# Second feed-forwards in pairs from their first block, weight splits first in each step, difference tiles 64 bytes off

## The chip, the cores and the metric

The kernel runs on one core of a Trainium2 chip. TensorE (PE) multiplies matrices from SBUF into PSUM; VectorE (DVE), ScalarE (ACT) and GpSimd (POOL) do elementwise work; SyncE (SP) issues most transfers, POOL some. The metric is the device time of one execution in microseconds. Before the change it is 2572.21 us, the median of 3 runs (2571.75 to 2572.4).

## The reference

Two layers of a hybrid decoder trunk on a 512 x 1024 fp32 input. Each layer is a half-step feed-forward, a mixer (attention and a state-space scan, whose branches are gated and merged) and a second half-step feed-forward; a last norm follows both layers.

```python
def reference(x, ...):
    for l in range(DEPTH):
        x = x + 0.5 * swiglu(rms_norm(x, ffn1_norm[l]), ffn1_w_up[l], ffn1_w_down[l])
        h = rms_norm(x, mix_norm[l])
        proj = h @ w_in[l]
        ...
        merged = jax.nn.sigmoid(gate_sb) * y_sb + jax.nn.sigmoid(gate_ssm) * y_ssm
        x = x + merged @ w_out[l]
        x = x + 0.5 * swiglu(rms_norm(x, ffn2_norm[l]), ffn2_w_up[l], ffn2_w_down[l])
    return rms_norm(x, final_norm)

def swiglu(h, w_up, w_down):
    gate, up = jnp.split(h @ w_up, 2, axis=-1)
    return (jax.nn.silu(gate) * up) @ w_down
```

D_MODEL is 1024 and the hidden width 2816, so a feed-forward has 22 hidden blocks of 128.

## The kernel before

**Tiles and precision.** x lies transposed in eight tiles of 128 channels x 512 tokens. Every fp32 product is made of three fp32r matmuls for each 128-block of the inner dimension (`mm3`, L331 to L333): high by high, high by low, low by high. So each weight unit and each input exists as a high and a low tile: whi and wlo, hhi and hlo. A unit of 128 x 1024 weights is 24 matmuls.

**Weight units.** `unit_order` lists all units of the program. `fetch` loads a unit (SP, into one of 3 wraw buffers), `convert` casts it to whi on ScalarE (L298) and, two ticks later, subtracts on VectorE to get wlo (L300); there are 3 buffers of each. When TensorE starts unit k, unit k+2 is converted, which has to wait until unit k-1 has freed its buffers.

**Blocks and pairs.** A hidden block of a feed-forward is either two units ("gate" and "up", 512 columns a matmul), or half of a pair. A pair computes gate and up of two blocks in seven products instead of eight half-width ones, each 24 matmuls of 256 columns: "11", "12", "s2", "s1", "s3", "s4", "22" in this order (`pair_of_blocks`). "11" and "12" and "s4" read the scaled input hhi, hlo; "s2", "s1", "s3" and "22" read the difference tiles th, tl, which `combine` makes from the x tiles (uv on ScalarE and VectorE, th by a cast on ScalarE L403, tl on VectorE L407). The weights of s1, s2, s3, s4 are sums: s1 and s3 are loaded as a base and a second matrix is added by an accumulating transfer that POOL issues (`onto`, L270); s2 and s4 are sums made on VectorE (`add`, L283), s4 in the tile of s2. `pairs_from` says from which block on a feed-forward uses pairs: block 6 in layer 0's first, block 2 in the others. `SLICES` cuts the 22 blocks into 8, 8 and 6; after each slice come eight "down" units that add to x.

**What sets the order.** The program is written in one order by hand. Side work (norm pieces, conversions, combines) are generators in the list `side`; `tick`, called once per three matmuls of `dense` (six in a pair's product), goes through the list in order and lets each due task emit its next instructions. Which of two tasks due in the same tick stands first on an engine is its place in the list; `spawn` puts a task at the end, or at the head with first=True. Each engine then works through its own queue in order.

**Norms.** The norm factor rs is not applied to the input but to the results (g, c), so products of the raw scaled input can start before it is known. `norm_end` (L530) sums the squares by two matmuls into pt (L541) that read rs and sq, the high and low part of acc. `dt_stage` (L809) makes decay sums in each mixer; its matmul L849 transposes sq (cum) into pt.

**Places.** hhi, hlo, whi, wlo and the act tiles start 96 bytes past a multiple of 256 in SBUF; th, tl and uv, in a pool on the right side (`open_t`), 224 past.

Of the kernel before, what the change touches and what calls it, by code (L numbers as in the profile page):

```python
# [12 lines left out]
ALU = mybir.AluOpType  # L13
# [4 lines left out]
P = 128  # L18
# [3 lines left out]
KB = DM // P  # L22
# [90 lines left out]

def pairs_from(layer, f):

    return 6 if (layer, f) == (0, 1) else 2


def unit_order(layer):

    def ffn(f):
        for s, (j0, j1) in enumerate(SLICES):
            for j in range(j0, j1):
                if j < pairs_from(layer, f):
                    yield (layer, f, "gate", j), KB
                    yield (layer, f, "up", j), KB
                elif j % 2 == 0:
                    for part in SEVEN:
                        yield (layer, f, "pair", j, part), KB
            for m in OUT_ORDER:  # L130
                yield (layer, f, "down", s, m), j1 - j0
# [32 lines left out]
class Builder:  # L164
# [7 lines left out]
    def __init__(self, ctx, tc, xT, wflat, par, taps, out):  # L172
        self.tc, self.nc = tc, tc.nc
        self.ctx = ctx
        self.xT, self.wflat, self.par, self.taps, self.out = xT, wflat, par, taps, out
        self.units, _ = all_units()
        self.keys = list(self.units)
        self.pos = 0
        self.raw, self.loaded = [], []
        self.count = 0  # L180
        self.side = []
        self.xd = None
        self.now, self.burst, self.free = 0, -1, {}
        self.sums, self.early, self.summed = {}, {}, 0
        for i, key in enumerate(self.keys):
            if key[2:] == ("gate", 0):
                first = i + 4
            if "pair" in key and key[-1] in ("s1", "s3"):
                self.early.setdefault(max(first, i - (5 if key[-1] == "s1" else 4)), []).append(key)
        self.logs = True  # L190

# [61 lines left out]
    def fetch(self, i):  # L253
        key = self.keys[i]
        raw = None
        if "pair" not in key or key[-1] in ("11", "12", "22"):
            raw = self.t(self.wraw, [P, KB * P], "wraw")
            self.nc.sync.dma_start(raw[:, :self.units[key][1] * P], self.stored(key))
            if key[-1] in ("11", "12"):
                self.sums[key] = raw  # L260
        self.raw.append(raw)
        for key in self.early.get(i, ()):
            raw = self.t(self.sx, [P, KB * P], key[-1], bufs=2)
            self.nc.sync.dma_start(raw, self.stored(key[:-1] + ("s1",)))
            self.spawn(self.onto(key, raw), 9)

    def onto(self, key, raw):

        src = self.stored(key[:-1] + ("22" if key[-1] == "s1" else "11",))
        self.nc.gpsimd.dma_start(raw, src, accum_op=ALU.add)  # L270
        self.sums[key] = raw
        yield 1

    def add(self, key):

# [10 lines left out]
    def convert(self, i):  # L286
# [5 lines left out]
        if key[-1] in ("s1", "s3"):  # L292
            raw = self.sums[key] if key[-1] == "s1" else self.sums.pop(key)
        elif key[-1] in ("s2", "s4"):
            raw = self.sums[key[:-1] + ("s2",)]
        hi = self.t(self.wsp, [P, KB * P], "whi", F32R)
        lo = self.t(self.wsp, [P, KB * P], "wlo", F32R)
# [1 line left out]
        yield 2  # L299
        nc.vector.tensor_tensor(lo[:, :n], raw[:, :n], hi[:, :n].bitcast(F32), op=ALU.subtract)  # L300
        self.loaded[i] = (hi, lo)

    def ahead(self, look=LOOK):

        last = len(self.keys) - 1
        while len(self.loaded) <= min(self.pos + look, last):
# [1 line left out]
            while len(self.raw) <= i:  # L308
                self.fetch(len(self.raw))
            self.loaded.append(None)  # L310
            self.spawn(self.convert(i))
        while len(self.raw) <= min(self.pos + self.AHEAD, last) and len(self.raw) - len(self.loaded) < 2:
            self.fetch(len(self.raw))
        for i in range(self.summed, min(self.pos + self.LOOK + 1, last) + 1):
            if self.keys[i][-1] in ("s2", "s4"):
                self.spawn(self.add(self.keys[i]))
            self.summed = i + 1

# [65 lines left out]
    def combine(self, k, gain):  # L384
# [11 lines left out]
        yield 1  # L396
        nc.vector.scalar_tensor_tensor(v[:, b], u[:, a], -1.0, v[:, b], op0=ALU.mult, op1=ALU.subtract)
        nc.vector.scalar_tensor_tensor(v[:, a], v[:, b], -1.0, v[:, a], op0=ALU.mult, op1=ALU.subtract)
        yield 2
        two = []  # L400
        for t in (u, v):
            two.append(self.t(self.tp, [P, SEQ], "th", F32R, bufs=KB))
            nc.scalar.copy(two[-1], t)  # L403
            yield 2
        for i, t, hi in zip((k, m), (u, v), two):
            lo = self.t(self.tp, [P, SEQ], "tl", F32R, bufs=KB)
            nc.vector.tensor_tensor(lo, t, hi.bitcast(F32), op=ALU.subtract)  # L407
# [176 lines left out]
    def pair_of_blocks(self, base, fp, two):  # L584
# [2 lines left out]

        nc, half, n = self.nc, SEQ // 2, KB // 2
        a, b = slice(0, half), slice(half, SEQ)
        lower, upper = self.h[:n], self.h[n:]  # L590
# [44 lines left out]

        up1, up2 = [], []
        g1, g2 = (self.t(fp, [P, SEQ], "g", bufs=4) for _ in range(2))
        product(chain, "11", lower, a, True)
        nc.scalar.copy(g1, chain)
        product(ps2, "12", upper, a, True)  # L640
        nc.vector.tensor_tensor(g1, g1, ps2, op=ALU.add)  # L641
        self.spawn(activate(g1, up1, a))
        assert None not in self.diff
        product(chain, "s2", diff[n:], b, False)
        nc.scalar.copy(g2, chain)
        product(ps3, "s1", diff[:n], a, True)
# [5 lines left out]
        product(ps3, "s4", upper, b, False)  # L652
# [104 lines left out]
    def ffn(self, layer, f, gain, gain_next):  # L757
        tc = self.tc
        with tc.tile_pool(name=f"act{layer}{f}", bufs=8, reuse_waits="tile") as ap, \
                tc.tile_pool(name=f"sx{layer}{f}", bufs=2, reuse_waits="tile") as self.sx, \  # L760
                tc.tile_pool(name=f"ffn{layer}{f}", bufs=3, reuse_waits="tile") as fp:
            self.gated = {}
            for s, (j0, j1) in enumerate(SLICES):
                act = []
                last = s == len(SLICES) - 1
                for j in range(j0, j1):
                    if j % 2 == 0:
# [1 line left out]
                        act += [tuple(t[:, i * SEQ:(i + 1) * SEQ] for t in two) for i in range(2)]  # L769
                    if j >= pairs_from(layer, f):  # L770
                        if j % 2 == 0:
                            self.pair_of_blocks((layer, f, "pair", j), fp, two)
# [36 lines left out]
    def dt_stage(self, layer):  # L809
# [36 lines left out]
        yield 2  # L846
        nc.scalar.activation(left, left, AF.Exp)
        pt = self.t(self.ptr, [P, SEQ], "pt")
        nc.tensor.transpose(pt[:n, :P], cum, self.ident)  # L849
# [558 lines left out]
    def close_t(self):  # L1408
        self.tpool.__exit__(None, None, None)
        self.tp = None  # L1410

    def build(self):
# [141 lines left out]
```

## Time and profile before

| | |
|---|---|
| median of 3 runs | 2572.21 us |
| profiled execution | 2571.97 us |
| its span | 2570.2 us |
| granted TensorE clock | 0.998 |
| first feed-forward of layer 0, span time | 0 to 352 us |
| mixer of layer 0, with its output stage from 897.28 | 352 to 940.80 us |
| second feed-forward of layer 0 | 940.80 to 1283.03 us |
| first feed-forward of layer 1 | 1283.03 to 1626.5 us |
| mixer of layer 1, with its output stage from 2171.55 | to 2215.07 us |
| second feed-forward of layer 1 | 2215.07 us to the end |

A profile comes from one execution. Its page gives busy time by engine, the chain of work that ended last, the costliest groups, and the waits of an engine with what ended them. A timeline row is: start in us, duration in us, engine, line, operation, output<-inputs, shape, count, and in brackets idle time before it and what ended it. Matmuls overlap, so the pace of TensorE is read from start to start, not from durations.

### The profile page before, as it was taken

What the parts mean: (1) busy time and instruction counts of PE and PEld (TensorE: products, weight loads), DVE (VectorE), ACT (ScalarE), POOL (GpSimd) and SP (SyncE); (2) the same over time, 40 slices, a digit from 0 to 9 for tenths busy, and PEclk for the clock granted to TensorE, in tenths of its full rate; (3) what the DMA queues carried; (4) which work ended last, traced back from release to release, by engine and by line L of the source; (5) the groups of instructions that cost most, each with busy time, mean ns of one, the idle gap of its engine ahead of it and who ended that gap; (6) DMA issues with size and microseconds to landing.
All of it is one profiled execution on the core that took longest, in us unless ns stands there. A gap on an engine that the chain in (4) does not pass through costs nothing.

```text
span 2570.2 us, 38025 instructions
## 1 busy us (share of the span) xinstructions
PE 2558.0 (100%) x15032; PEld 2290.0 (89%) x15032; DVE 1726.6 (67%) x2251; ACT 1279.1 (50%) x2103; POOL 518.8 (20%) x646
## 2 busy tenths in 40 slices
PE   9999999999999999999999999999999999999998
PEld 8898988888898889899998989888888888899997
DVE  8576875666564478586885858756666644876766
ACT  6343556665554255343553535566555533543444
POOL 0121201054342002121121312011533310122120
PEclk9999999999999999999999999999999999999999
DMA  6454442233333454555364544423333334456452
GB/s 190 131 157 139 132 139 88 87 123 103 105 109 105 141 161 134 164 140 163 108 181 140 156 140 130 141 79 102 117 98 104 116 113 142 153 142 167 140 162 82
DMA packets 104659, 335.76 MB, mean 131 GB/s; under 512 B 11872, under 2 KB 15392, under 8 KB 104480
## 3 DMA queue, kind: packets, MB, share of 16 engines
q1 hardware_dynamic: 92672, 292.84, 34.2%
q0 software_dynamic: 10944, 39.85, 8.7%
q8 instruction: 118, 1.93, 0.3%
q10 hardware_dynamic: 864, 0.64, 0.1%
q14 instruction: 61, 0.50, 0.1%
HBM read 320.60 MB, written 12.68 MB: 130 GB/s over the span
## 4 chain that ended last, share of the span: by engine, by line
PE 97%; DVE 2%; ACT 1%; DMA 0%; issue 0%; SPq 0%; DVEq 0%; ACTq 0%
PE mm L331 27%; PE mm L333 27%; PE mm L332 27%; PE pa L333 3%; PE pa L332 3%; PE pa L331 3%; PE pa L1186 2%; PE pa L1188 1%; PE pt L864 1%; PE pt L1171 1%; PE pt L1169 1%; PE pa L469 0%; PE pa L864 0%; PE pa L981 0%; DVE wlo L300 0%; PE pt L333 0%
## 5 line engine op out<-in xcount | busy, mean ns | idle before, releaser
L298 ACT CAST whi<-wraw 128x1024 fp32r<-128x1024 f32 (+3 forms) x440 | 435.2, 989 | 597.3 <-PE mm L333 488.2
L300 DVE TENSOR_TENSOR wlo<-wraw,whi 128x1024 fp32r<-128x1024 f32 (+3 forms) x440 | 538.1, 1223 | 204.7 <-ACT whi L298 203.6
L331 PE MATMUL mm<-hhi,whi 128*128 128x512 f32 (+1 forms) x1584 | 564.6, 356 | 0.0
L333 PE MATMUL mm<-hlo,whi 128*128 128x512 f32 (+1 forms) x1584 | 553.5, 349 | 0.4 <-DVE hlo L515 0.4
L332 PE MATMUL mm<-hhi,wlo 128*128 128x512 f32 (+1 forms) x1584 | 552.5, 349 | 0.0
L333 PEld LDWEIGHTS mm<-hlo,whi 128*128 128x128 f32 x1584 | 299.7, 189 | 40.4 <-DVE hlo L515 0.8
L332 PEld LDWEIGHTS mm<-hhi,wlo 128*128 128x128 f32 x1584 | 300.1, 189 | 35.2 <-DVE wlo L300 0.4
L331 PEld LDWEIGHTS mm<-hhi,whi 128*128 128x128 f32 x1584 | 300.1, 189 | 34.5 <-ACT hhi L513 0.4
L300 DVE TENSOR_TENSOR wlo<-s,whi 128x1024 fp32r<-128x1024 f32 x152 | 235.4, 1563 | 60.1 <-ACT whi L298 60.1
L331 PE MATMUL mm<-act,whi 128*128 128x512 f32 (+1 forms) x710 | 273.9, 386 | 0.0
L333 PE MATMUL mm<-act,whi 128*128 128x512 f32 (+1 forms) x710 | 273.9, 386 | 0.0
L332 PE MATMUL mm<-act,wlo 128*128 128x512 f32 (+1 forms) x710 | 273.9, 386 | 0.0
L331 PE MATMUL mm<-th,whi 128*128 128x256 f32 x912 | 257.1, 282 | 0.0
L333 PE MATMUL mm<-tl,whi 128*128 128x256 f32 x912 | 256.7, 281 | 0.0
L332 PE MATMUL mm<-th,wlo 128*128 128x256 f32 x912 | 256.5, 281 | 0.0
L634 POOL TENSOR_TENSOR g<-g,rs 128x512 f32<-128x512 f32 x76 | 132.9, 1748 | 552.5 <-DVE g L641 533.7
L298 ACT CAST whi<-s 128x1024 fp32r<-128x1024 f32 x152 | 159.3, 1048 | 102.2 <-PE mm L333 60.5
L660 DVE SCALAR_TENSOR_TENSOR x<-mm,x 128x512 f32<-128x512 f32 x93 | 64.1, 689 | 195.9 <-PE mm L333 195.9
L270 POOL DMA_DIRECT2D s<-in_wflat_dram x76 | 66.0, 868 | 616.1 <-DMA s<-in_wflat_dram 330.9
L331 PEld LDWEIGHTS mm<-th,whi 128*128 128x128 f32 x912 | 172.1, 189 | 0.0
L332 PEld LDWEIGHTS mm<-th,wlo 128*128 128x128 f32 x912 | 171.8, 188 | 0.0
L333 PEld LDWEIGHTS mm<-tl,whi 128*128 128x128 f32 x912 | 171.7, 188 | 0.0
(304 smaller groups left out, 5076.9 us busy)
## 6 DMA issues: line engine op xcount, KB each, us to landing
wraw<-in_wflat_dram SPq DMA_DIRECT2D x328, 512.0 KB, 3.6
s<-in_wflat_dram SPq DMA_DIRECT2D x76, 512.0 KB, 4.7
s<-in_wflat_dram POOLq DMA_DIRECT2D x76, 512.0 KB, 7.7
wraw<-in_wflat_dram SPq DMA_DIRECT2D x88, 384.0 KB, 3.0
cumb<-cum_d SPq DMA_DIRECT2D x16, 768.0 KB, 4.8
xd<-x SPq DMA_DIRECT2D x16, 256.0 KB, 3.1
wraw<-in_wflat_dram SPq DMA_DIRECT2D x16, 256.0 KB, 2.9
x<-xd SPq DMA_DIRECT2D x16, 256.0 KB, 3.7
```

What stands on the lines that cost most here:

```text
L270: self.nc.gpsimd.dma_start(raw, src, accum_op=ALU.add)
L298: nc.scalar.copy(hi[:, :n], raw[:, :n])
L300: nc.vector.tensor_tensor(lo[:, :n], raw[:, :n], hi[:, :n].bitcast(F32), op=ALU.subtract)
L331: mm(ps, a[0], b[0], start=start, stop=False, **kw)
L332: mm(ps, a[1], b[0], start=False, stop=False, **kw)
L333: mm(ps, a[0], b[1], start=False, stop=stop, **kw)
L634: eng.tensor_tensor(r, r, self.rs[:, cols].unsqueeze(1).to_broadcast([P, 2, half]), op=ALU.mult)
L660: self.nc.vector.scalar_tensor_tensor(x, pd, 0.5, x, op0=ALU.mult, op1=ALU.add)
L864: self.nc.tensor.transpose(pt[:, cs], src[:, cs], self.ident)
L1169: nc.tensor.matmul(pc[:, :P], bt[:, span(c)], ct[:, span(c)], start=True, stop=True)
L1171: nc.tensor.matmul(pu, btok[:, c, :], xws[c].rearrange("p h d -> p (h d)"), start=True, stop=True)
L1186: nc.tensor.matmul(py[:, i * HD:(i + 1) * HD], decs[c][:, i, :], xdts[c][:, i, :], start=True, stop=True)
```

## The change

It has five edits.

1. `pairs_from` gives 0 for the second feed-forward of each layer, so blocks 0 and 1 become a pair there. Pairs 0 and 2 are then computed in turns (`leading`): "11" and "12" of pair 0, "11" and "12" of pair 2, the other five of pair 0, the other five of pair 2. `pair_of_blocks` becomes a generator that stops behind "12" and ticks until all difference tiles exist. Pair 0 sums no weights on VectorE: s2 is a base load and two accumulating transfers, and s4 a third one onto the same tile, sent once s2 is split.
2. `ahead` spawns each conversion at the head of the task list, so in a tick that has several tasks due the weight split stands first.
3. The last `combine` has gaps of one tick instead of two.
4. `dt_stage` waits three ticks instead of two before its transpose.
5. The pool of the s tiles moves to the right side behind tpool, and a pool "rim" of 320 bytes ahead of tpool shifts th, tl and uv from 224 to 160 bytes past a multiple of 256.

```diff
 def pairs_from(layer, f):
-    return 6 if (layer, f) == (0, 1) else 2
+    return {(0, 1): 6, (1, 1): 2}.get((layer, f), 0)
+
+def leading(layer, f):
+    return [(layer, f, "pair", j, part) for j, parts in
+            ((0, SEVEN[:2]), (2, SEVEN[:2]), (0, SEVEN[2:]), (2, SEVEN[2:])) for part in parts]
...
         for s, (j0, j1) in enumerate(SLICES):
+            if s == 0 and not pairs_from(layer, f):
+                for key in leading(layer, f):
+                    yield key, KB
+                j0 = 4
...
-            if "pair" in key and key[-1] in ("s1", "s3"):
+            if key[2:] == ("pair", 0, "11"):
+                first = i - 4
+                for n, part in enumerate(("s2", "s1", "s3")):
+                    self.early.setdefault(first + n, []).append(key[:-1] + (part,))
+            elif "pair" in key and key[-2] and key[-1] in ("s1", "s3"):
...
     def onto(self, key, raw):
-        src = self.stored(key[:-1] + ("22" if key[-1] == "s1" else "11",))
-        self.nc.gpsimd.dma_start(raw, src, accum_op=ALU.add)
-        self.sums[key] = raw
-        yield 1
+        for part in {"s1": ("22",), "s3": ("11",), "s2": ("22", "11"), "s4": ("12",)}[key[-1]]:
+            self.nc.gpsimd.dma_start(raw, self.stored(key[:-1] + (part,)), accum_op=ALU.add)
+            if key[-1] != "s2" or part == "11":
+                self.sums[key] = raw
+            yield 9
...
         elif key[-1] in ("s2", "s4"):
+            while key[2:] == ("pair", 0, "s4") and key not in self.sums:
+                yield 1
             raw = self.sums[key[:-1] + ("s2",)]
...
         self.loaded[i] = (hi, lo)
+        if key[2:] == ("pair", 0, "s2"):
+            self.spawn(self.onto(key[:-1] + ("s4",), raw), 2)
...
-            self.spawn(self.convert(i))
+            self.spawn(self.convert(i), first=True)
...
-        yield 2
+        gap = 1 if m == KB - 1 else 2
+        yield gap
...
-        assert None not in self.diff
+        yield
+        while None in self.diff:
+            self.tick()
         product(chain, "s2", diff[n:], b, False)
...
         nc.scalar.activation(ecb, pt[:, n:2 * n], AF.Exp)
-        yield 2
+        yield 3
...
     def open_t(self):
+        self.rim = self.tc.tile_pool(name=self.name("rim"), bufs=1, side="right", reuse_waits="tile")
+        self.t(self.rim.__enter__(), [P, 80], "rim")
         self.tpool = self.tc.tile_pool(name=self.name("tpool"), bufs=2, side="right", reuse_waits="tile")
         self.tp = self.tpool.__enter__()
+        self.spool = self.tc.tile_pool(name=self.name("spool"), bufs=2, side="right", reuse_waits="tile")
+        self.sx = self.spool.__enter__()
```

**ScalarE at the first pair of layer 0's second feed-forward.** Before, pair 2 is the first. Names: s1, s2, s3 are the summed weights, g and c the results, and the COPY rows empty PSUM.

```order
L298 CAST whi_1633_9080<-s2_1624_9039 128x1024
L419 CAST act_1588_8883<-a_1632_9078 128x512
L639 COPY g_1630_9070<-mm_1627_9067 128x512
L298 CAST whi_1636_9113<-s1_1593_8889 128x1024
L298 CAST whi_1639_9145<-s3_1594_8891 128x1024
L645 COPY g_1631_9071<-mm_1627_9067 128x512
L612 ACTIVATE g_1630_9070<-g_1630_9070 128x512
L298 CAST whi_1643_9181<-s2_1624_9039 128x1024
L648 COPY c_1645_9204<-pa_1629_9069 128x512
```

Now, with pair 0 first (the cast that reads s2 for the second time is that of the s4 weights):

```order
L315 CAST whi_1637_9083<-s3_1538_8604 128x1024
L666 COPY g_1603_8908<-mm_1599_8904 128x512
L315 CAST whi_1639_9117<-s2_1523_8521 128x1024
L631 ACT_TABLE_LOAD
L631 ACTIVATE g_1602_8907<-g_1602_8907 128x512
L631 ACTIVATE g_1621_8993<-g_1621_8993 128x512
L669 COPY c_1641_9144<-pa_1601_8906 128x512
L315 CAST whi_1642_9152<-wraw_1636_9075 128x1024
```

Between the cast of s4 and the copy to c there now stand a table load and two activations; the cast itself reads what a POOL transfer has added to.

**POOL at the same place**, behind the last work of the mixer (gny); the DMA rows are accumulating transfers, the other rows scale a result by rs. Now:

```order
L1255 TENSOR_TENSOR gny_1385_7816<-ss_1335_7575,small_142 128x4
L284 DMA s2_1523_8521<-in_wflat_dram 128x1024
L284 DMA s1_1530_8561<-in_wflat_dram 128x1024
L284 DMA s2_1523_8521<-in_wflat_dram 128x1024
L284 DMA s3_1538_8604<-in_wflat_dram 128x1024
L284 DMA s1_1609_8946<-in_wflat_dram 128x1024
L284 DMA s2_1523_8521<-in_wflat_dram 128x1024
L653 TENSOR_TENSOR g_1602_8907<-g_1602_8907,rs_1633_9062 128x512
L653 TENSOR_TENSOR g_1621_8993<-g_1621_8993,rs_1633_9062 128x512
```

Before, two accumulates (s1 and s3 of pair 2) stood between gny and the first scaling; now there are six, the last of them for s4 of pair 0.

**VectorE at the end of layer 0's second feed-forward**, on the last residual block (x). Before:

```order
L660 SCALAR_TENSOR_TENSOR x_8501<-mm_12226,x_8501 128x512
L407 TENSOR_TENSOR tl_12299<-uv_12219,th_12256 128x512
L407 TENSOR_TENSOR tl_12307<-uv_12220,th_12265 128x512
L515 SCALAR_TENSOR_TENSOR hlo_12302<-x_8501,par_107,hhi_12301 128x512
L300 TENSOR_TENSOR wlo_12294<-wraw_12186,whi_12293 128x1024
```

And now:

```order
L681 SCALAR_TENSOR_TENSOR x_8506<-mm_12334,x_8506 128x512
L427 TENSOR_TENSOR tl_12403<-uv_12327,th_12364 128x512
L317 TENSOR_TENSOR wlo_12397<-wraw_12294,whi_12396 128x1024
L427 TENSOR_TENSOR tl_12412<-uv_12328,th_12373 128x512
L535 SCALAR_TENSOR_TENSOR hlo_12406<-x_8506,par_114,hhi_12405 128x512
```

The split (wlo) moved from behind hlo to ahead of the second tl.

**TensorE at the transpose of `dt_stage`** in layer 0 (pt<-ident,sq); the pa rows are attention scores, the mm rows the next weight unit. Before:

```order
L332 MATMUL pa_4500<-yt_4087,yt_4145 128x128
L333 MATMUL pa_4500<-yt_4088,yt_4144 128x128
L849 MATMUL pt_4509<-ident,sq_4394 96x128
L331 MATMUL mm_4512<-hhi_3573,whi_4384 128x512
L332 MATMUL mm_4512<-hhi_3573,wlo_4385 128x512
```

And now:

```order
L351 MATMUL pa_4505<-yt_4095,yt_4153 128x128
L352 MATMUL pa_4505<-yt_4096,yt_4152 128x128
L350 MATMUL mm_4514<-hhi_3578,whi_4382 128x512
L351 MATMUL mm_4514<-hhi_3578,wlo_4383 128x512
L352 MATMUL mm_4514<-hlo_3579,whi_4382 128x512
L875 MATMUL pt_4529<-ident,sq_4399 96x128
L350 MATMUL mm_4514<-hhi_3589,whi_4382 128x512
```

The transpose stands behind the first three matmuls of the unit instead of ahead of them.

More of the change, by code (lines that the diff above doesn't have):

```diff
@@ L130, in ffn @@
             for m in OUT_ORDER:
-                yield (layer, f, "down", s, m), j1 - j0
+                yield (layer, f, "down", s, m), j1 - SLICES[s][0]
     yield from ffn(1)
@@ L262, in fetch @@
         for key in self.early.get(i, ()):
-            raw = self.t(self.sx, [P, KB * P], key[-1], bufs=2)
+            raw = self.t(self.sx, [P, KB * P], key[-1], bufs=1 if key[-1] == "s2" else 2)
             self.nc.sync.dma_start(raw, self.stored(key[:-1] + ("s1",)))
@@ L314, in ahead @@
         for i in range(self.summed, min(self.pos + self.LOOK + 1, last) + 1):
-            if self.keys[i][-1] in ("s2", "s4"):
+            if self.keys[i][-1] in ("s2", "s4") and self.keys[i][-2]:
                 self.spawn(self.add(self.keys[i]))
@@ L403, in combine @@
             nc.scalar.copy(two[-1], t)
-            yield 2
+            yield gap
         for i, t, hi in zip((k, m), (u, v), two):
@@ L589, in pair_of_blocks @@
         a, b = slice(0, half), slice(half, SEQ)
-        lower, upper = self.h[:n], self.h[n:]
         diff = self.diff
@@ L637, in pair_of_blocks @@
         g1, g2 = (self.t(fp, [P, SEQ], "g", bufs=4) for _ in range(2))
-        product(chain, "11", lower, a, True)
+        product(chain, "11", self.h[:n], a, True)
         nc.scalar.copy(g1, chain)
-        product(ps2, "12", upper, a, True)
+        product(ps2, "12", self.h[n:], a, True)
         nc.vector.tensor_tensor(g1, g1, ps2, op=ALU.add)
         self.spawn(activate(g1, up1, a))
-        assert None not in self.diff
+        yield
+        while None in self.diff:
+            self.tick()
         product(chain, "s2", diff[n:], b, False)
@@ L651, in pair_of_blocks @@
         self.spawn(normed_up(c))
-        product(ps3, "s4", upper, b, False)
+        product(ps3, "s4", self.h[n:], b, False)
         nc.vector.tensor_tensor(g2, g2, ps3, op=ALU.add)
@@ L759, in ffn @@
         with tc.tile_pool(name=f"act{layer}{f}", bufs=8, reuse_waits="tile") as ap, \
-                tc.tile_pool(name=f"sx{layer}{f}", bufs=2, reuse_waits="tile") as self.sx, \
                 tc.tile_pool(name=f"ffn{layer}{f}", bufs=3, reuse_waits="tile") as fp:
@@ L763, in ffn @@
             for s, (j0, j1) in enumerate(SLICES):
-                act = []
+                act, quads = [], []
                 last = s == len(SLICES) - 1
@@ L771, in ffn @@
                         if j % 2 == 0:
-                            self.pair_of_blocks((layer, f, "pair", j), fp, two)
+                            quads.append(self.pair_of_blocks((layer, f, "pair", j), fp, two))
+                            next(quads[-1])
+                        if j % 2 == 0 and (j or pairs_from(layer, f)):
+                            for quad in quads:
+                                for _ in quad:
+                                    pass
+                            quads = []
                         continue
@@ L845, in dt_stage @@
         nc.scalar.activation(ecb, pt[:, n:2 * n], AF.Exp)
-        yield 2
+        yield 3
         nc.scalar.activation(left, left, AF.Exp)
@@ L1403, in open_t @@
     def open_t(self):
+        self.rim = self.tc.tile_pool(name=self.name("rim"), bufs=1, side="right", reuse_waits="tile")
+        self.t(self.rim.__enter__(), [P, 80], "rim")
         self.tpool = self.tc.tile_pool(name=self.name("tpool"), bufs=2, side="right", reuse_waits="tile")
         self.tp = self.tpool.__enter__()
+        self.spool = self.tc.tile_pool(name=self.name("spool"), bufs=2, side="right", reuse_waits="tile")
+        self.sx = self.spool.__enter__()
     def close_t(self):
+        self.spool.__exit__(None, None, None)
         self.tpool.__exit__(None, None, None)
+        self.rim.__exit__(None, None, None)
         self.tp = None
```

## The prediction

> **What bounds the kernel now.** I read the page's busy table first, then its chain of work that ended last, then the waits of TensorE.
>
> ```profile
> PE 2558.0 (100%) x15032; PEld 2290.0 (89%) x15032; DVE 1726.6 (67%) x2251; ACT 1279.1 (50%) x2103; POOL 518.8 (20%) x646
> PE 97%; DVE 2%; ACT 1%; DMA 0%; issue 0%; SPq 0%; DVEq 0%; ACTq 0%
> PE pt L1432 <- DVE ones L485: 1.1, 1, 1.1
> PE pt L849 <- DVE sq L842: 0.8, 2, 0.4
> PE mm L333 <- DVE hlo L515: 0.4, 1, 0.4
> PE pt L707 <- ACT g L695: 0.2, 1, 0.2
> ```
>
> TensorE is busy for the whole span, it is 97% of the chain, and its listed waits come to 2.5 us out of 2570. So the time falls only if TensorE gets less to do or does it at another pace, and rises wherever a wait is added. Every edit is priced in TensorE time.
>
> **Part 1: two blocks become a pair in each second feed-forward.** The view that cuts time into stretches shows the start of layer 0's second feed-forward: four units of a gate and an up, then a pair.
>
> ```profile
> 940.80:948.96 8.16, 8.16 (x37) 6.76 (x36) 7.20 (x13) 6.03 (x9) 1.79 (x2) 1.00 0.91 287
> 949.41:963.01 13.60, 13.60 (x61) 11.27 (x60) 10.10 (x14) 7.18 (x9) 0.00 (x0) 1.00 0.66 169
> 963.01:983.03 20.02, 20.02 (x169) 20.01 (x168) 15.61 (x14) 10.49 (x13) 6.40 (x5) 1.00 0.59 155
> ```
>
> The columns are length, busy time of PE, PEld, DVE, ACT and POOL with counts, granted clock, DMA share and GB/s. The 0.45 us between the first two stretches are the norm's two matmuls, which stay. Blocks 0 and 1 take 8.16 + 13.60 = 21.76 us as four units of 24 matmuls of 512 columns (0.2267 us each). As a pair they are seven products of 24 matmuls of 256 columns, which the third row prices at 20.02 us. Removed: 1.74 us, twice: **-3.48 us**. Work is halved in columns but not in time, which is why it is so little: 168 x 0.1192 against 96 x 0.2267.
>
> **Part 2: what the new start waits for.** I laid the new order of each engine on these durations, from 940.80. Products of 24 take 2.86 to 2.88 us: pair 0's "11" and "12" to 946.6, pair 2's "11" to 949.4, the norm's matmuls to about 950.1, pair 2's "12" to 953.0, then "s2" to 955.9, "s1" to 958.7, "s3" to 961.6, "s4" after that.
>
> The norm's second matmul needs sq, which VectorE made at 947.13 in the profile.
>
> ```profile
> 947.13 0.68 DVE L537 TENSOR_TENSOR sq<-acc,rs 128x512 fp32r<-128x512 f32 x1
> 948.86 1.29 DVE L407 TENSOR_TENSOR tl<-uv,th 128x512 fp32r<-128x512 f32 x2
> ```
>
> The shorter steps put one more split (1.22 us in the rows of part 3, 1.14 from start to start) and the sum of the first two products (0.69 us, as the x rows of the same shape in part 3) ahead of sq: it ends near 947.13 + 0.68 + 1.14 + 0.69 = 949.6, where 949.4 is wanted. I take 0.2 us. The last tl moves by the same 1.83 us and ends near 952.0; "s2" wants it at 953.0: no wait.
>
> The new wait is that of "s4". In pair 0 its weights are no longer summed on VectorE: a POOL transfer adds "12" onto the s2 tile, and may go only once s2 is split, about 951.0. The weights' cast on ScalarE waits for its landing, and behind that cast stand the table load, two Silus and the copy c, in this order. "s4" writes the PSUM tile that the copy empties, so TensorE waits for the whole row.
>
> ```profile
> DMA to landing us min/median/max: 5.1/7.7/11.6
> 952.33 1.06 ACT L298 CAST whi<-wraw 128x1024 fp32r<-128x1024 f32 x1 [0.79 <-PE mm L333]
> 953.41 1.28 ACT L571 ACT_TABLE_LOAD   x1
> 954.70 0.63 ACT L571 ACTIVATE g<-g 128x512 f32<-128x512 f32 x1
> 966.09 0.59 ACT L639 COPY g<-mm 128x512 f32<-128x512 f32 x1 [1.30 <-PE mm L333]
> ```
>
> The first row is that of POOL's accumulating transfers, 76 of them. Issue at 951.0 plus the median 7.7 is 958.7. Cast, table, two Silus and copy take 1.06 + 1.28 + 2 x 0.63 + 0.59 = 4.2, less some overlap at the seams: 4.0. So c is free at 962.7 and "s4" starts 1.1 us late. At 5.1 it costs nothing (6.6 is where it starts to), at 11.6 it costs 5.0. VectorE's split of s4 waits with the cast, and behind it stand the next sum and the split of "22", each with a product's time to spare. On POOL the transfer stands ahead of the two g times rs, which wait for rs until 955.4 anyway. SP carries one base load more, issued in the output stage, four units ahead. So 0.2 + 1.1, twice: **+2.6 us** (0 to +10.4).
>
> **Part 3: splits first, and the gap of the last combine.** Most splits pass hlo, sums or products that TensorE needs later. The exception I found is where the next feed-forward starts on the last residual block, at 1283.03.
>
> ```profile
> 1286.39 0.69 DVE L660 SCALAR_TENSOR_TENSOR x<-mm,x 128x512 f32<-128x512 f32 x1
> 1287.00 1.28 DVE L407 TENSOR_TENSOR tl<-uv,th 128x512 fp32r<-128x512 f32 x2
> 1288.20 0.75 DVE L515 SCALAR_TENSOR_TENSOR hlo<-x,par,hhi 128x512 fp32r<-128x512 f32 x1
> 1288.86 1.22 DVE L300 TENSOR_TENSOR wlo<-wraw,whi 128x1024 fp32r<-128x1024 f32 x1
> ...
> 1288.23 0.40 PE L332 MATMUL mm<-hhi,wlo 128*128 128x512 f32 x1
> 1289.00 0.50 PE L333 MATMUL mm<-hlo,whi 128*128 128x512 f32 x1 [0.38 <-DVE hlo L515]
> 1289.33 0.40 PE L331 MATMUL mm<-hhi,whi 128*128 128x512 f32 x1
> ...
> 1290.04 0.39 PE L331 MATMUL mm<-hhi,whi 128*128 128x512 f32 x1
> ...
> 1292.78 0.39 PE L541 MATMUL pt<-rs,nones 128*128 128x512 f32 x1
> 1293.19 0.50 PE L541 MATMUL pt<-sq,nones 128*128 128x512 f32 x1
> 1293.53 0.40 PE L331 MATMUL mm<-hhi,whi 128*128 128x512 f32 x1
> ```
>
> VectorE is behind here, and TensorE waits for the last hlo (0.77 us from one start to the next where 0.23 is normal). The new order runs x, tl, wlo, tl, hlo: a split of 1.14 us moves ahead, so hlo and TensorE come 1.14 later. What follows in the norm had a wait of its own (0.41 and 0.34 to the next starts for 0.23 each), and that 0.29 is won back: **+0.85 us**, once. The transition of layer 0's first feed-forward into the mixer has slack, and at the program's end nothing follows. In the mixers the splits pass attention rows; TensorE's list of waits has no row of VectorE there but L849's. I take 0, with ends of -1 and +1 (a list of 0.8 us bounds the gain, a split of 1.14 the loss).
>
> **Part 4: the dt transpose goes behind three matmuls.**
>
> ```profile
> 463.23 0.28 PE L332 MATMUL pa<-yt,yt 128*128 128x128 f32 x1
> 463.35 0.27 PE L333 MATMUL pa<-yt,yt 128*128 128x128 f32 x1
> 464.03 0.32 PE L849 MATMUL pt<-ident,sq 128*96 128x128 f32 x1 [0.41 <-DVE sq L842]
> 464.11 0.48 PE L331 MATMUL mm<-hhi,whi 128*128 128x512 f32 x1
> ```
>
> From start to start stand 0.68 us where the step before took 0.12; the idle time given is 0.41. I take 0.5, between 0.41 and 0.56. The three matmuls that now come first last 0.68 and hide it; what then waits for cum has room. Twice -0.5: **-1.0 us**.
>
> **Part 5: difference tiles 64 bytes off.** This touches the pace of the 96 matmuls a pair that read th or tl: 40 pairs after the change, 3840 matmuls, so each nanosecond is 3.84 us. In before, hhi, hlo and the weights lie at 96 modulo 256 and th, tl at 224; after, th and tl lie at 160. First matmuls of "11" (48 follow), of "s2", of "s4" behind three products, and of the next pair:
>
> ```profile
> 983.03 0.28 PE L331 MATMUL mm<-hhi,whi 128*128 128x256 f32 x1
> 988.79 0.28 PE L331 MATMUL mm<-th,whi 128*128 128x256 f32 x1
> ...
> 997.33 0.28 PE L331 MATMUL pa<-hhi,whi 128*128 128x256 f32 x1
> ```
>
> Inputs at the weights' own offset run at 5.76 / 48 = 120.0 ns, those 128 bytes off at 8.54 / 72 = 118.6. So where a tile lies may matter, and no row has 64. Back to 120.0 would cost 5.4 us. Far ends: half of a 512-column matmul's 226.7 ns, 113.3, would save 20 us; the slow stretch at 1289.33 to 1290.04 above (237 ns, 4% over its normal pace) would cost as much as 18. Both rows near it lie within 1.4 ns: I take **0**, and keep both ends with little weight.
>
> The Trainium skill (SBUF — State Buffer, Specifications (TRN2)) gives SBUF lines of 16 bytes, and under Who interferes with whom it says: "PE and ACT never wait on anyone." By that, 0, 64 and 128 bytes are alike and this term is nothing; the trace has 120.0 against 118.6, so the rule doesn't explain all that is seen, but no run here shows 64.
>
> **Sum**, against the profiled execution's 2571.97 us (span 2570.2 and 1.8 around it; 0.24 under the median 2572.21): -3.48 + 2.6 + 0.85 - 1.0 = -1.0. On the median: **2571.2 us**.
>
> **Rivals.** (a) *The difference matmuls run faster at 64 bytes.* For it: pace does follow the tile in the rows; against: the step from 0 to 128 bought 1.4 ns only, and 1.1 ns more are needed to show. At 115 ns it gives 3.6 x 3.84 = 14, so 2557. Chance 0.24. (b) *Slower: the accumulate for "s4" lands late.* For it: the two issued at this very place took longer than the median, where DMA share was 0.91 and VectorE busy for 7.20 of 8.16 us, and pair 0 adds five accumulates.
>
> ```profile
> s<-in_wflat_dram POOLq DMA_DIRECT2D x1, 512.0 KB, 8.6
> s<-in_wflat_dram POOLq DMA_DIRECT2D x1, 512.0 KB, 11.0
> ```
>
> Against: these two were issued at 945.14 and 946.85, and the 0.66 of the next stretch is calmer. At 11.0 "s4" stands 4.4 us late, at 11.6 5.0; in both layers the latter is +7.8 on the forecast: 2579. The sum loses its sign where each stall is 0.5 us over the 1.1 (landing after 8.2 us), and it shows from 3.1 over (after 10.8). Chance 0.10. The Trainium skill (SBUF — State Buffer, SBUF: two separate sides) has a rule that speaks for (b): a DMA issued from GpSimd has its descriptors written there, and stands while VectorE holds the shared port. By that rule it would land past the median here, since VectorE stands full; the 8.6 and 11.0 agree, though the DMA share could do as much. (c) *Slower: the matmuls lose pace at 64 bytes.* From 1.6 ns it shows; at 122 ns it gives +13, 2584. Against it: the row at 0 bytes, the worst, costs 5.4. Chance 0.08. (d) *Nothing comes of it:* the start gives back all of the 1.74 (a stall of 1.7 for 1.3): 2572. Chance 0.10, within 0.2%.
>
> **How the numbers follow.** 0.2% is 5.1 us, about what a measurement of this kernel can tell from no change. The forecast has 0.48, and lies within it with (d): 0.58. Faster is (a), 0.24; slower is (b) and (c), 0.18. The likeliest case's own range is 2567 to 2576; (a) between 2557 and 2566 and the low part of (b) and (c) are needed for eight in ten, so 2560 to 2578.
>
> **What would show it.** Right: a pair 0 and 2 that take 2 x 20.02 us plus about 1.3; a listed wait of "s4"'s first matmul on c; the L849 wait gone; hlo's wait near 1.5 us after layer 0's second feed-forward; th products at 2.85 us. Wrong: th products away from 2.85 (part 5), a wait of "s4" above 3 us or none (part 2), or a new TensorE wait for VectorE in a mixer (part 3).

## The result and the profile after

The changed kernel takes 2567.76 us (median of 21 runs, 2566.56 to 2569.38), the kernel before 2571.75 us (21 runs, 2571.26 to 2572.40). The ratio is 0.9985, with a 95% interval of 0.9978 to 0.9991: 4.0 us or 0.15% faster. The forecast was 1.0 us faster. The profiled execution took 2567.14 us with a span of 2565.4 us, 4.8 us under that of before; the stage figures below are from these two executions. The difference of the two is 0.8 us larger than that of the medians, since one lies 0.6 us under its median and the other 0.2 us over.

The page's busy line, the first line of its chain, and the view of what TensorE waited for (us in total, times, longest), after the change:

```profile
PE 2551.3 (99%) x15176; PEld 2291.4 (89%) x15176; DVE 1728.9 (67%) x2257; ACT 1281.3 (50%) x2115; POOL 553.7 (22%) x662
PE 94%; DVE 3%; ACT 1%; issue 1%; DMA 0%; POOL 0%; SPq 0%; DVEq 0%; ACTq 0%; POOLq 0%
PE mm L351 <- DVE wlo L317: 1.2, 1, 1.2
PE pt L1464 <- DVE ones L505: 1.1, 1, 1.1
PE pa L1007 <- DVE short L444: 0.8, 2, 0.4
PE mm L352 <- DVE hlo L535: 0.6, 1, 0.6
PE pa L350 <- ACT c L669: 0.3, 1, 0.3
PE pt L728 <- ACT g L716: 0.2, 1, 0.2
```

TensorE is still the bound. Its wait for the dt transpose is gone, and three waits are new: 1.2 us for a weight split near the program's start, 0.4 us in each mixer's attention (short), and 0.3 us for c in front of "s4" (in layer 1). The wait for hlo grew from 0.4 to 0.6 us. To see where the time went I took the same matmul's start in both traces and followed the difference (after less before) through the program. The column "change" is what a stage added to it.

| stage | change, us | forecast, us |
|---|---|---|
| first products and norm, to the first pair | +0.83 | 0 |
| attention of the two mixers (short) | +0.59, +0.60 | 0 |
| dt transpose and what follows it | -0.68, -0.57 | -0.5, -0.5 |
| rest of the two mixers | -0.25 | 0 |
| start of the two second feed-forwards, pairs 0 and 2 | -1.35, -1.42 | -0.44, -0.44 |
| layer 0's second into layer 1's first feed-forward | -0.37 | +0.85 |
| all other pairs of the four feed-forwards | -0.54, -0.59, -0.66, -0.59 | 0 |
| sum | -5.0 | -1.0 |

The spans differ by 0.2 us less, since the end behind the last matmul grew by that much.

The stretches that hold pairs 0 and 2 and the norm's two matmuls, in the columns of the view by stretches (length, then busy time of PE, PEld, DVE, ACT and POOL, clock, DMA share, GB/s):

```profile
940.91:981.80 40.89, 40.87 (x340) 40.36 (x339) 36.87 (x41) 27.84 (x37) 14.96 (x10) 1.00 0.62 157
2212.09:2252.89 40.80, 40.46 (x340) 39.96 (x339) 36.55 (x41) 27.86 (x37) 14.96 (x10) 1.00 0.64 162
```

Before, the same work took 8.16 + 0.45 + 13.60 + 20.02 = 42.23 us. Two pairs of 20.02 and the norm would be 40.49, so waits and slow steps, less what the quicker difference matmuls gave, come to 0.3 to 0.4 us, where the forecast had 1.3. The dt transpose, which had stood 0.68 us behind its predecessor, now follows in 0.24 (timeline rows of TensorE: start, duration, line, operation):

```profile
464.85 0.40 PE L352 MATMUL mm<-hlo,whi 128*128 128x512 f32 x1
465.09 0.27 PE L875 MATMUL pt<-ident,sq 128*96 128x128 f32 x1
```

The pace of the difference matmuls changed as well. Here are the first matmul of "s2" and the first of "s4", three th products of 24 later, in the pair at 1002 us:

```profile
1007.52 0.28 PE L350 MATMUL mm<-th,whi 128*128 128x256 f32 x1
1016.00 0.29 PE L350 MATMUL pa<-hhi,whi 128*128 128x256 f32 x1
```

8.48 us for 72 is 117.8 ns a matmul, for 118.6 before. Over the whole trace the mean from start to start of the th products that write mm went from 118.74 to 117.76 ns.

### The profile page after: what moved, and what is told of

Its sections match the earlier page's. It is cut to its first block, busy times and chain, and to the rows that moved or that the text cites. A ratio compares the mean times of both kernels' runs of the same rounds, so it can differ in the third digit from the quotient of the medians.

```text
span 2565.4 us, 38502 instructions
## 1 busy us (share of the span) xinstructions
PE 2551.3 (99%) x15176; PEld 2291.4 (89%) x15176; DVE 1728.9 (67%) x2257; ACT 1281.3 (50%) x2115; POOL 553.7 (22%) x662
## 4 chain that ended last, share of the span: by engine, by line
PE 94%; DVE 3%; ACT 1%; issue 1%; DMA 0%; POOL 0%; SPq 0%; DVEq 0%; ACTq 0%; POOLq 0%
PE mm L350 26%; PE mm L352 26%; PE mm L351 26%; PE pa L350 3%; PE pa L352 3%; PE pa L351 3%; PE pa L1212 2%; PE pa L1214 1%; DVE wlo L317 1%; PE pt L890 1%; PE pt L1197 1%; PE pt L1195 1%; PE pa L890 0%; ACT whi L315 0%; PE pa L1007 0%
## 5 line engine op out<-in xcount | busy, mean ns | idle before, releaser
L350 PE MATMUL mm<-hhi,whi 128*128 128x512 f32 (+1 forms) x1552 | 548.8, 354 | 0.0
L352 PE MATMUL mm<-hlo,whi 128*128 128x512 f32 (+1 forms) x1552 | 537.8, 347 | 0.6 <-DVE hlo L535 0.6
L351 PE MATMUL mm<-hhi,wlo 128*128 128x512 f32 (+1 forms) x1552 | 536.7, 346 | 1.2 <-DVE wlo L317 1.2
L653 POOL TENSOR_TENSOR g<-g,rs 128x512 f32<-128x512 f32 x80 | 165.1, 2066 | 552.2 <-DVE g L660 507.1
L350 PE MATMUL mm<-th,whi 128*128 128x256 f32 x960 | 268.9, 280 | 0.0
L351 PE MATMUL mm<-th,wlo 128*128 128x256 f32 x960 | 267.9, 279 | 0.0
L352 PE MATMUL mm<-tl,whi 128*128 128x256 f32 x960 | 267.8, 279 | 0.0
L284 POOL DMA_DIRECT2D s<-in_wflat_dram x86 | 75.4, 876 | 622.2 <-DMA s<-in_wflat_dram 553.1
L315 ACT CAST whi<-s 128x1024 fp32r<-128x1024 f32 x160 | 167.8, 1049 | 74.8 <-PE mm L352 52.8
L352 PEld LDWEIGHTS mm<-tl,whi 128*128 128x128 f32 x960 | 180.4, 188 | 0.0
```

Of the source, the lines that this page charges most:

```text
L284: self.nc.gpsimd.dma_start(raw, self.stored(key[:-1] + (part,)), accum_op=ALU.add)
L315: nc.scalar.copy(hi[:, :n], raw[:, :n])
L350: mm(ps, a[0], b[0], start=start, stop=False, **kw)
L351: mm(ps, a[1], b[0], start=False, stop=False, **kw)
L352: mm(ps, a[0], b[1], start=False, stop=stop, **kw)
L653: eng.tensor_tensor(r, r, self.rs[:, cols].unsqueeze(1).to_broadcast([P, 2, half]), op=ALU.mult)
```

## The experiments

Twelve kernels ran, each beside the kernel before (2571.6 to 2571.8 us in these runs). Diffs are against the changed kernel unless said otherwise. No run leaves out edit 3 (the gap of the last combine) or edit 4 (the dt transpose) alone; what is said of these two is read from the traces.

**e1: the tiles back at 128 bytes from the weights.**

```diff
-        self.t(self.rim.__enter__(), [P, 80], "rim")
+        self.t(self.rim.__enter__(), [P, 64], "rim")
```

> The change with the rim of 256 instead of 320 bytes: th, tl, uv (and the s tiles) lie 224 past a multiple of 256 again, as before the change; all else stays. Theory (the place of the difference tiles sets their pace): the th matmuls go back from 117.75 ns (mm) and 117.65 (pa) to 118.7 and 118.6, the 256-column hhi matmuls from 119.98 and 120.07 to 119.85 and 119.4; 3840 x 0.97 - 1920 x 0.13 - 960 x 0.69 = about +2.8 us against the change, so 2570.5. Rival (the pace follows from the other order of the program, or from the runs): the paces stay and the time stays at 2567.8.

Measured: 2570.67 us, 2.9 more than the change. The same two places in its timeline:

```profile
1009.14 0.28 PE L350 MATMUL mm<-th,whi 128*128 128x256 f32 x1
1017.69 0.28 PE L350 MATMUL pa<-hhi,whi 128*128 128x256 f32 x1
```

8.55 us for 72: 118.75 ns. The place of the tiles accounts for 2.9 of the 4.0 us.

**e4: the kernel before with the tiles at 64 bytes alone** (a pool of 64 bytes ahead of its tpool).

```diff
     def open_t(self):
+        self.rim = self.tc.tile_pool(name=self.name("rim"), bufs=1, side="right", reuse_waits="tile")
+        self.t(self.rim.__enter__(), [P, 16], "rim")
```

> The kernel before with a rim of 64 bytes alone, which puts th, tl and uv at 160 past a multiple of 256 (64 past the weights' place instead of 128). Theory: th pace 117.75 for 118.7 on 3648 matmuls, hhi 256-column matmuls a little slower: -3.5 + 0.9 = -2.7 us against before, 2569.1. Rival: the pace in the changed kernel came with the moved s tiles or the order, and this one stays at 2571.8.

Measured: 2569.19 us, 2.5 under before, with th products at 117.87 ns. The same edit gives nearly the same gain in the other order of the program.

**e3: no pairs on blocks 0 and 1.**

```diff
-    return {(0, 1): 6, (1, 1): 2}.get((layer, f), 0)
+    return {(0, 1): 6}.get((layer, f), 2)
```

> The change with the second feed-forwards' blocks 0 and 1 as normal units again (pairs from block 2). Theory (a pair saves 1.74 us of TensorE and its start costs about 0.4): the two starts lose 1.35 and 1.42 us, so +2.7, 2570.5. Rival (the start pays for its saving with waits elsewhere, in the output stage of the mixer or later pairs): under +1.

Measured: 2570.11 us, 2.35 over the change. The pairs are worth 1.2 us in each second feed-forward, a little less than the traces gave.

**e2: splits at the end of the task list.**

```diff
-            self.spawn(self.convert(i), first=True)
+            self.spawn(self.convert(i))
```

> The change with conversions spawned at the end of the task list again. Theory (splits first cost more than they give): TensorE's wait for wlo of 1.2 us near 24 us goes, and the 0.6 us at the attention's first transposed sum in each mixer; the wait for hlo behind layer 0's second feed-forward goes back to what it was, about +0.4: together about -2, so 2566. Rival (early splits are what keeps the start of the interleaved pairs free of waits): new TensorE waits for wlo in the first five products of pair 0 of over 1 us each layer, and a time of 2568 or more.

Measured: 2570.08 us, 2.3 over the change. The time is the rival's, but the waits stand elsewhere than it said. TensorE's largest waits in this kernel are one of each of these two in each layer; below them are the two matmuls of layer 0:

```profile
PE mm L350 <- ACT whi L315: 2.5, 2, 1.3
PE mm L351 <- DVE wlo L317: 1.2, 2, 0.6
965.25 0.35 PE L350 MATMUL mm<-th,whi 128*128 128x256 f32 x1 [1.27 <-ACT whi L315]
974.67 0.38 PE L351 MATMUL mm<-th,wlo 128*128 128x256 f32 x1 [0.58 <-DVE wlo L317]
```

The first stands behind "s4" and is the start of "22", the last product of pair 0. The second is in "s3" of pair 2. Here is VectorE ahead of the first, in e2 and then in the change:

```profile
960.06 2.21 DVE L298 TENSOR_TENSOR s<-s,wraw 128x1024 f32<-128x1024 f32 x1
962.19 2.32 DVE L317 TENSOR_TENSOR wlo<-wraw,whi 128x1024 fp32r<-128x1024 f32 x1
964.43 0.68 DVE L671 TENSOR_TENSOR c<-mm,c 128x512 f32<-128x512 f32 x1
```

```profile
959.44 2.20 DVE L298 TENSOR_TENSOR s<-s,wraw 128x1024 f32<-128x1024 f32 x1
962.68 1.23 DVE L317 TENSOR_TENSOR wlo<-wraw,whi 128x1024 fp32r<-128x1024 f32 x1 [1.03 <-ACT whi L315]
963.82 0.68 DVE L671 TENSOR_TENSOR c<-mm,c 128x512 f32<-128x512 f32 x1
```

"22" adds to the PSUM tile that VectorE reads for c, so it can't start before c is done. In e2 that is at 965.11, 0.14 us before the matmul. The view names a cast that ends in the same moment, but that cast makes weights of a later product (the weights of "22" were cast at 960.57); in e12 below, the view puts a wait of 1.3 us of the same matmul in layer 1 down to c. In the change c ends at 964.50, and "22" starts at 964.73 without a wait. VectorE's order is the same in both. The split takes 2.32 us in one and 1.23 in the other, with POOL scaling g beside both, and the runs do not show why; so how the spawn order brings about this wait stays open. The second wait is plain. VectorE again, e2 and then the change:

```profile
972.79 0.68 DVE L444 TENSOR_TENSOR act<-a,act 128x512 fp32r<-128x512 f32 x1
973.40 2.35 DVE L317 TENSOR_TENSOR wlo<-s,whi 128x1024 fp32r<-128x1024 f32 x2
```

```profile
972.01 1.22 DVE L317 TENSOR_TENSOR wlo<-s,whi 128x1024 fp32r<-128x1024 f32 x1
973.15 0.69 DVE L444 TENSOR_TENSOR act<-a,act 128x512 fp32r<-128x512 f32 x1
```

The split that "s3" needs (in e2 the first of the two in its row) stands behind act in e2 and ahead of it in the change. From e2 to the change the traces lose 1.45 us at the wait near 24 us and 0.6 in each attention, and gain 2.1 and 2.3 at the two starts, 0.7 in each mixer near a wait of TensorE for bT, and about 0.7 elsewhere.

The gains of e1, e3 and e2 (2.9, 2.35 and 2.3 us) don't add up to the 4.0 us of the change, because the early splits pay mostly where the new pairs start. By the stage table the pairs' two starts gave 2.8 us, and the early splits took 2.0 back at the program's start and in the attention. With the -0.37 us behind layer 0's second feed-forward, these two edits together brought about 1 us; the tiles' place and the dt transpose brought most of the rest.

**e5 and e10: early splits where they pay.** e5 spawns first for feed-forward units past the first eight units of the program; e10 for all units past these but q, k and v.

```diff
-            self.spawn(self.convert(i), first=True)
+            self.spawn(self.convert(i), first=self.keys[i][1] in (1, 2) and self.pos > 8)
...
+            self.spawn(self.convert(i), first=self.keys[i][1] not in ("q", "k", "v") and self.pos > 8)
```

> The change with conversions spawned first only for the units of the feed-forwards, past the first eight units of the program. Theory (the early splits pay at the pairs' starts alone): the wait of 1.2 us near 24 us and the 0.6 us in each attention go, the short starts of the interleaved pairs stay; the mixers lose 0.3 each elsewhere: 1.2 + 1.2 - 0.7 = -1.7, 2566.1. Rival (the mixers' early splits carry more than they cost): 2567.8 or more.

> The change with conversions spawned first except for the q, k and v units and past the first eight units of the program. Theory (early splits help wherever TensorE's next unit is what VectorE and ScalarE are late with, and hurt only at the program's start and in the attention's first sums): the 1.3 us near 29 us and the 0.6 us in each attention go, and the 0.5 us a mixer that splits for the feed-forwards alone lost comes back: 2567.8 - 1.3 - 1.2 = 2565.3. Rival (the 0.5 us of the mixers come from the q, k, v units themselves): 2566.4.

Measured: 2566.37 and 2564.70 us. Both are near their theories' times. Against the change, e10's trace has 1.45 us less at the wait near 24 us and 0.6 less in each attention; in the view of waits the rows for wlo, for short and for c are gone:

```profile
PE pt L1464 <- DVE ones L505: 1.1, 1, 1.1
PE mm L352 <- DVE hlo L535: 0.6, 1, 0.6
PE pt L728 <- ACT g L716: 0.2, 1, 0.2
```

e5 loses about 0.7 us in each mixer, where 0.3 was expected, near a wait of TensorE for bT that e10 does not have: the early splits of the mixers' other units are worth that much.

**e7 and e8: other distances.** The rim has 352 bytes (32 from the weights' place) and 128 bytes (0 from it).

```diff
-        self.t(self.rim.__enter__(), [P, 80], "rim")
+        self.t(self.rim.__enter__(), [P, 88], "rim")
...
+        self.t(self.rim.__enter__(), [P, 32], "rim")
```

> The change with a rim of 352 bytes: th, tl at 128 past a multiple of 256, 32 past the weights. If the pace falls steadily from 0 to 64 bytes of distance (120.0, then 117.7), 118.8 ns and +4.2 us, 2572; if only the 64-byte line counts, 120.0 or 117.7.

> The change with a rim of 128 bytes: th, tl at 96, the weights' own place. Theory: th matmuls run as the hhi ones do, 120.0 ns: 3840 x 2.25 = +8.6 us less 0.9 for the hhi matmuls behind them, 2575.5. Rival (the pace differs by kind of input, not by place): 117.7 and no change.

Measured: 2567.06 and 2575.27 us. The two places in e8:

```profile
1010.19 0.28 PE L350 MATMUL mm<-th,whi 128*128 128x256 f32 x1
1018.83 0.28 PE L350 MATMUL pa<-hhi,whi 128*128 128x256 f32 x1
```

8.64 us for 72: 120.0 ns, what hhi has at the weights' own place. So it is the place against the weights and not the kind of input, and e7's forecast of a steady slope (118.8 ns at 32 bytes, 2572 us) missed, while its other one (117.7) came close: 120.0 at 0, 117.85 at 32, 117.76 at 64, 118.75 at 128.

**e6 and e11: the raw inputs 64 bytes off as well.** 192 bytes between hlo and the weights put these, act and mhi at 32; hhi, hlo, th and tl at 96. In e6 yt and ohi are at 96 too; e11 brings them to 32 and has the splits of e10.

```diff
         self.hp = enter(tc.tile_pool(name="hp", bufs=KB))
+        self.t(enter(tc.tile_pool(name="pad", bufs=1)), [P, 48], "pad")
...
-        self.t(self.rim.__enter__(), [P, 80], "rim")
+        self.t(self.rim.__enter__(), [P, 32], "rim")
...
-            self.t(edge, [P, 96], "edge")
+            self.t(edge, [P, 48], "edge")
```

> The change with 192 bytes between the inputs hhi, hlo and the weights, and a rim of 128 bytes: weights and act tiles lie at 32 past a multiple of 256, hhi, hlo, th, tl and the yt tiles at 96, that is 64 past the weights. Theory (what counts is the distance from the weights' place): th matmuls stay at 117.7 ns and the 2880 hhi matmuls of 256 columns go from 120.0 to 117.8: -6.3 us, 2561.5, and the 512-column ones, if they gain alike, another few us. Rival (what counts is the place itself, 160 being good and 96 bad): th goes to 120 ns, hhi stays, +8.6 us, 2576.

> The kernel of e10 with the places of e6 (hhi, hlo, th, tl 64 past the weights), but with the yt, ohi and mhi tiles moved to the weights' place. Theory (256-column matmuls gain by a distance of 64, 512-column ones lose by it): yt and ohi go from 229 ns back to 226.8, 750 matmuls or -1.6 us against e6; hhi keeps 117.5 (256 columns) and 229.4 (512): 2567.8 - 1.6 and the 2.5 of the splits = 2563.7. Rival (the 512-column loss comes from elsewhere): yt and ohi stay at 229, 2565.3.

Measured: 2567.81 and 2564.16 us. In e6 the 256-column hhi matmuls did go from 120.0 to 117.5 ns and th stayed at 117.4, so distance and not the place itself set this; but those of 512 columns got slower, hhi from 228.0 to 229.5 and yt from 226.8 to 228.9, and took the gain back. In e11 yt is at 226.8 again. So a distance of 64 bytes helped the 256-column matmuls here and hurt those of 512 columns.

**e12: hhi 32 bytes and th 64 bytes off.** Weights, act, mhi, yt and ohi at 64, hhi and hlo at 96, th and tl at 128; splits as in e10.

```diff
+        self.t(enter(tc.tile_pool(name="pad", bufs=1)), [P, 56], "pad")
...
+        self.t(self.rim.__enter__(), [P, 88], "rim")
...
+            self.t(edge, [P, 40], "edge")
```

> As e11 with 32 bytes between the weights' place and hhi, hlo (weights at 64, hhi at 96 past a multiple of 256) and 64 to th, tl. If a distance of 32 costs 512-column matmuls less than 64 does (226.7 to 228 for 229.4) and serves 256-column ones as well as it served th (117.8): 2562 or less. If 512 columns lose as with 64: 2564 as e11.

Measured: 2558.74 us (4 runs), ratio 0.9949 (0.9934 to 0.9964): the fastest of all, 12.9 us under before. Only a small part is for the reason given: hhi of 256 columns went to 116.9 ns, but hhi of 512 columns is slower than ever (233.2 ns). Most comes from th, which runs at another pace. "11", "s2" and "s4" start at:

```profile
1002.71 0.28 PE L350 MATMUL mm<-hhi,whi 128*128 128x256 f32 x1
1008.32 0.28 PE L350 MATMUL mm<-th,whi 128*128 128x256 f32 x1
1016.48 0.28 PE L350 MATMUL pa<-hhi,whi 128*128 128x256 f32 x1
```

8.16 us for 72 is 113.3 ns, at the same distance of 64 bytes that gave 117.8 in the change.

**e13: everything on multiples of 64.** As e12, with hhi and hlo at 128.

```diff
+        self.t(enter(tc.tile_pool(name="padl", bufs=1)), [P, 8], "padl")
         self.hp = enter(tc.tile_pool(name="hp", bufs=KB))
-        self.t(enter(tc.tile_pool(name="pad", bufs=1)), [P, 56], "pad")
+        self.t(enter(tc.tile_pool(name="pad", bufs=1)), [P, 48], "pad")
```

> The kernel of e12 with hhi and hlo moved by 32 bytes, to 128 past a multiple of 256: weights at 64, hhi, hlo, th, tl at 128, all of them on multiples of 64 and all inputs of pairs 64 past the weights. Theory (two things count, the distance from the weights, and that both lie on multiples of 64): hhi of 256 columns goes from 117.0 to the 114.3 that th has in e12, and hhi of 512 columns from 233.2 to the 229.5 of a distance of 64, or better: 2880 x 2.7 + 2700 x 3.7 = -18 us, 2541; with 512 columns at 226.8 some 7 less. Rival (th's 114.3 came from something else that e12 changed, such as the place of the products' other inputs before them): hhi of 256 columns stays at 117 or more, and the time at 2550 or above.

Measured: 2564.45 us; th went back to 117.6 ns although neither th nor the weights had moved:

```profile
1007.51 0.28 PE L350 MATMUL mm<-th,whi 128*128 128x256 f32 x1
1015.99 0.28 PE L350 MATMUL pa<-hhi,whi 128*128 128x256 f32 x1
```

Only hhi and hlo had moved, which the products before read. The theory that a distance of 64 bytes and places on multiples of 64 give the quick pace falls; the rival holds.

## Why the prediction came out as it did

The time lies in the range and the sign is right, within 0.2% as forecast; but the sum was 3.0 us off by the medians and 4.0 by the traces, and three of its five parts were wrong in part. That it came so near is partly luck: 2.0 us of losses that it did not have, at the program's start and in the attention, hide a third of the 6 us that it left out or overpriced on the other side. Of the three signs that it named for being wrong, two were seen: th products at 2.83 us instead of 2.85, and a new wait for VectorE in the mixers. The wait of "s4" was short, 0.2 and 0.5 us.

**Part 1, the pair's saving (-1.74 each), held** as far as the waits let it show. e3 gives 1.2 net in each second feed-forward, and the trace 1.35 and 1.42, some 0.2 of it pace.

**Part 2, the new waits (1.3 each), was mis-sized.** The transfer for "s4" was taken at the median of 7.7 us from issue to landing. It took 5.4 and 5.7 in the two layers:

```profile
s<-in_wflat_dram POOLq DMA_DIRECT2D x1, 512.0 KB, 5.4
s<-in_wflat_dram POOLq DMA_DIRECT2D x1, 512.0 KB, 5.7
```

In the ten further kernels with this start it took 5.2 to 5.9. Issue was at 951.25, where the forecast had 951.0, so the landing came at 956.6, while ScalarE was at another copy until 956.70, and no longer set the end. ScalarE's rows in the change show what did:

```profile
956.11 0.59 ACT L666 COPY g<-mm 128x512 f32<-128x512 f32 x1 [1.78 <-PE mm L352]
956.68 1.05 ACT L315 CAST whi<-s 128x1024 fp32r<-128x1024 f32 x1
957.75 1.28 ACT L631 ACT_TABLE_LOAD   x1
959.04 0.63 ACT L631 ACTIVATE g<-g 128x512 f32<-128x512 f32 x1
960.60 0.64 ACT L631 ACTIVATE g<-g 128x512 f32<-128x512 f32 x1 [0.92 <-POOL g L653]
961.13 0.57 ACT L669 COPY c<-pa 128x512 f32<-128x512 f32 x1
```

The chain of cast, table, two Silus, copy was right, but inside it the second Silu waited 0.92 us for POOL, whose two scalings took 4.38 us together; the forecast gave these scalings no price. "s4" started 0.30 us (layer 1: 0.61) behind the matmul before it, where 0.12 is normal. Rival (b), a late landing, has nothing for it. The rule of the Trainium skill (SBUF — State Buffer, SBUF: two separate sides) that the prediction put behind it is stated there for a VectorE operation in a 2-port mode, and the Trainium skill (SBUF — State Buffer, Who interferes with whom) says that a tensor_tensor has no such mode. The prediction applied it to a busy VectorE as such. VectorE was busy for 36.87 of 40.89 us here, all of it in rows of TENSOR_TENSOR and SCALAR_TENSOR_TENSOR, and the transfer took 5.4.

**Part 3, splits first (+0.85), failed in its step on the last residual block.** It held x where it was and counted hlo's delay from there. VectorE's rows ahead of x, before:

```profile
1283.99 0.75 DVE L515 SCALAR_TENSOR_TENSOR hlo<-x,par,hhi 128x512 fp32r<-128x512 f32 x1
1284.66 1.22 DVE L300 TENSOR_TENSOR wlo<-wraw,whi 128x1024 fp32r<-128x1024 f32 x1
1285.79 0.69 DVE L528 TENSOR_TENSOR acc<-acc,sq 128x512 f32<-128x512 f32 x1
```

And now, on to the last hlo:

```profile
1281.04 1.22 DVE L317 TENSOR_TENSOR wlo<-wraw,whi 128x1024 fp32r<-128x1024 f32 x1
1282.17 0.74 DVE L535 SCALAR_TENSOR_TENSOR hlo<-x,par,hhi 128x512 fp32r<-128x512 f32 x1
1282.84 0.68 DVE L548 TENSOR_TENSOR acc<-acc,sq 128x512 f32<-128x512 f32 x1
1283.44 0.68 DVE L681 SCALAR_TENSOR_TENSOR x<-mm,x 128x512 f32<-128x512 f32 x1
1284.04 0.68 DVE L427 TENSOR_TENSOR tl<-uv,th 128x512 fp32r<-128x512 f32 x1
1284.64 1.22 DVE L317 TENSOR_TENSOR wlo<-wraw,whi 128x1024 fp32r<-128x1024 f32 x1
1285.77 0.68 DVE L427 TENSOR_TENSOR tl<-uv,th 128x512 fp32r<-128x512 f32 x1
1286.38 0.74 DVE L535 SCALAR_TENSOR_TENSOR hlo<-x,par,hhi 128x512 fp32r<-128x512 f32 x1
```

The feed-forward's first unit starts at 1281.20 here (1283.03 before), so x comes 2.24 us into it instead of 3.36: the split ahead of x had moved up as well, to before the previous hlo. What the split takes from hlo it has given to x, and hlo ends 5.92 us into the unit in both. Of the forecast only the end of the norm's wait behind it came true. The same part saw no loss in the mixers and did not look at the program's start; the traces show 0.59 and 0.60 and the wait of 1.2. e2 and e10 settle what the edit is worth: 2.3 us in all, and 3.1 more where it is left out of the opening and of q, k and v.

**Part 4, the dt transpose (-1.0), held** by the traces: -0.68 and -0.57 with what follows.

**Part 5, the pace (0, rival (a) at 14 us), had the mechanism in the rival and the size between:** 0.98 ns of 3840 matmuls, less some loss in the hhi products behind them. e1 and e4 give 2.9 and 2.5 us. The rows had shown that place matters (120.0 and 118.6); to call the term 0 was to take the middle of what was unknown for the likeliest. By the prediction's reading, the rule of the Trainium skill (SBUF — State Buffer, Who interferes with whom) that PE never waits on anyone made all distances alike. It speaks of engines that get in one another's way, and what was measured depends on two inputs of TensorE alone: 120.0, 117.85, 117.76 and 118.75 ns at 0, 32, 64 and 128 bytes.

## What to carry to other kernels

Where TensorE is the bound, read its pace from start to start for every kind of matmul, not from its waits: a move of an input by 64 bytes against its weights was worth as much here as a rewritten schedule, and is one line to try. A priority for one kind of work on a shared engine is to be priced at every place that it reaches, with the work that it moves up counted at both ends; then it can be kept where it pays. Where the sign of a sum hangs on how long one transfer takes, give it a range: here neither the program's median (7.7 us) nor the two transfers at the same place before (8.6 and 11.0) told the 5.4 and 5.7 that came.

## What the runs showed of the hardware that was not expected

The pace of the fp32r matmuls depended here on where the moving tile (the input that streams through, th or hhi) lies against the weights, and on the place of tiles that other products read. Means from start to start over whole traces, in ns, without the few steps that a wait made long (th products into mm, then hhi of 256 and of 512 columns; distances from the weights' place modulo 256):

| kernel | th, distance | th | hhi, distance | hhi 256 | hhi 512 |
|---|---|---|---|---|---|
| e8 | 0 | 119.99 | 0 | 119.95 | 228.0 |
| e7 | 32 | 117.85 | 0 | 119.86 | 228.0 |
| change | 64 | 117.76 | 0 | 119.98 | 228.0 |
| e1 | 128 | 118.75 | 0 | 119.86 | 228.0 |
| e11 | 64 | 117.50 | 64 | 117.57 | 229.6 |
| e13 | 64 | 117.57 | 64 | 117.62 | 229.5 |
| e12 | 64 | 114.44 | 32 | 116.94 | 233.2 |

At a distance of 64 a product of 24 runs either at about 117.7 or at about 113.3 ns, seldom between. In the change 3 of 158 th products ran at the faster pace, in e12 124 of 158, in e13 7 of 158. th and the weights lie in the same places in e12 and e13, so the place of hhi and hlo, which th products do not read, decides how often th gets the faster pace; that is shown for these two kernels. A reading that fits is that a product takes over a state from the one before it. The traces speak for this: in e12, where one th product stands directly behind another, 60 of 64 behind a fast one were fast and none of 18 behind a slow one. What the state is and what makes it was not tried, and why 512 columns lose at 32 and 64 bytes stays open too. The next to try would be hhi at the weights' place in e12: by this table it would save some 15 us on 2880 matmuls of 512 columns and cost 9 on 2880 of 256 (an estimate from the rows of e12 and the change), if th kept its pace, which no run shows.
